# Turning the convolved x: from products with the identity on TensorE to 32-row blocks on VectorE with a DRAM scratch

## The chip, the cores and the metric

The kernel runs on one core of one Trainium2 chip. The metric is the device time of one execution in microseconds (us), the median of several runs. The engines that run side by side on the core are TensorE (PE; its weight loads are listed apart as PEld), VectorE (DVE), ScalarE (ACT), GpSimd (POOL) and SyncE (SP, which here only issues DMAs). Each works through its own queue in order, and a semaphore tells one engine that another is done.

## The reference

A trunk of two layers over 256 tokens of width 2048: first a Mamba-2 SSD mixer, then sliding-window attention, each followed by a layer norm. The change lies in the SSD mixer. Its inner width of 4096 is 8 groups of 8 heads of 64; a chunk is 128 tokens, so there are two.

```python
zxbcdt = x @ w_in                       # z | x, B, C | dt
xbc = silu(causal_conv4(xbc) + conv_b)  # x, B, C
dt = softplus(dt_raw + dt_bias);  a = -exp(a_log)
x_c = xs * dt
y_diag = einsum("bcqgn,bcsgn->bgcqs", c_c, b_c) * decay_in  applied to x_c
y = y_diag + y_off + xs * d_skip
y = y * silu(z);  y = rms_norm over each group of 512 * norm_w
out = y @ w_out
```

`x_c` is summed over tokens s, so TensorE needs x with the tokens on the partitions, while the projection and the convolution give it with the channels on the partitions. That is the turn in question.

## The kernel before

**Weights and units.** All matrix products of the projections are done in fp32 split into a high and a low part (three products: high by high, low by high, high by low). A unit is a weight piece of 128x2048 (1 MB). `load_unit` loads it as two halves `wr` (5 buffers) on SP's queue; ACT writes the high part `wh` (line 133), VectorE subtracts it for the low part `wl` (line 134); 4 buffers each. `next_unit` keeps two units ahead of the one in use. A projection unit is 48 matmuls of 256 columns (lines 195 to 197) into one of 4 PSUM tiles `mm`; an output unit is 24 matmuls of 512 columns (lines 255 to 257) into two of them.

**A group.** `group(g)` runs 10 projection blocks: B, C, four blocks of x, four of z (in group 0 the four z first). Each block's PSUM goes through `conv_silu`: one ACT step (line 357), three taps on VectorE (line 359; the last one frees the PSUM tile), tanh on ACT (362), a closing step on VectorE (363). Between the blocks the output units of the group before are run, four per group. In the program groups take 14 units of 1 MB and 1.5 MB of decay rows.

**The steps of SSD** are put at block numbers of a hand-written plan (`at(t, step)`; t is 10 g plus an offset): `sum_decay` and `exp_decay` make the decays `e` on ACT from rows that a DRAM scratch `rscr` broadcasts; `cb` makes C by B on TensorE and multiplies it into `e` on VectorE; `tr` turns x: eight transposes (products with the identity `ident`, line 453) into two PSUM tiles `ax` and four scaled copies to SBUF tiles `xd` on VectorE (line 458, the scale is `dtx`, dt with a part of the decay); `ymm` computes y with `xd` as the stationary operand and `e` as the moving one (line 476: 16 matmuls of 64 columns, two per head pair side by side, each executed as two weight loads and two matmuls), then VectorE scales by `el` (481) and adds the skip term from `xs` (487); `gate` multiplies by z, squares and sums on POOL and splits y for the output product (506, 507); `norm` follows five blocks later. In groups 2 to 7 `cb` stands at block 4, `tr` at 7, `ymm` at 9. In group 0 they stand at 8, 12 and 13, which is already in group 1's blocks.

**What sets the order.** The plan and the calls give the program order; a scheduler then sets each engine's order from it and from its own estimate of when things are ready. Tiles of one tag share a number of buffers, and a new tile waits until the last reader of the buffer is done.

**Buffers that the change touches.** Tag `sm` has 7 buffers of 1 KB per partition, for the temporaries of `make_dt`, the four `xs` and the squares of `gate`; `xd` has 4 of 1 KB; `yz` one of 4 KB.

Of the kernel before, what the change touches and what calls it, by code (L numbers as in the profile page):

```python
# [8 lines left out]
F32 = mybir.dt.float32  # L9
# [3 lines left out]
ALU = mybir.AluOpType  # L13
AX = mybir.AxisListType

P = 128
S = 256
# [10 lines left out]
TD, TS, CB0 = 5, 5, 8  # L28
# [6 lines left out]

BLOCKS = list(range(10))
BLOCKS0 = [6, 7, 8, 9, 0, 1, 2, 3, 4, 5]
CB_AT, TR_AT, Y_AT, NSM = 4, 7, 9, 7
B_ORDER = [("q", 0), ("g", 0), ("q", 1), ("g", 1), ("o", 0), ("q", 2), ("g", 2), ("o", 1),
           ("q", 3), ("g", 3), ("o", 2), ("o", 3)]  # L40
ALPHA = (2.0 * 2) ** 0.25
# [16 lines left out]
def trunk(ctx: ExitStack, tc: tile.TileContext, A: dict, out: bass.AP, dbg=None):  # L58
    nc = tc.nc
# [12 lines left out]
    dram = pool("dram", space=bass.MemoryType.DRAM)  # L72
# [3 lines left out]
    def nm(s):  # L76
        uid[0] += 1
        return f"{s}_{uid[0]}"
# [4 lines left out]
    def ax_tile():  # L83
        return ax_ps.tile([P, 512], F32, tag="ax", name=nm("ax"), bufs=4)

    cc = cst.tile([P, 896], F32, tag="cc", name="cc")
    ident = cc[:, 0:128]
# [209 lines left out]
    rscr = dram.tile([P, S], F32, tag="rscr", name="rscr")  # L297

    def make_dt(ps):
        f = [ap.tile([P, S], F32, tag="sm", name=nm("f"), bufs=NSM) for _ in range(7)]  # L300
        u, e, rec, z, w, q, dt = [x[:] for x in f]
        nc.scalar.activation(u, ps[:, :S], AF.Identity, bias=pc[:, PC_DTB : PC_DTB + 1])
        nc.scalar.activation(e, u, AF.Abs)
        nc.scalar.activation(e, e, AF.Exp, scale=-1.0)
        aneg = ap.tile([P, 1], F32, tag="aneg", name="aneg")
        nc.scalar.activation(aneg[:], pc[:, PC_ALOG : PC_ALOG + 1], AF.Exp)
        nc.vector.tensor_scalar(aneg[:], aneg[:], -1.0, None, ALU.mult)
        nc.vector.tensor_scalar(rec, e, 2.0, None, ALU.add)
        nc.vector.reciprocal(rec, rec)
        nc.vector.tensor_tensor(z, e, rec, ALU.mult)  # L310
        nc.vector.tensor_tensor(w, z, z, ALU.mult)
        nc.vector.tensor_scalar(q, w, 1.0 / 15.0, None, ALU.mult)
        nc.vector.tensor_scalar(z, z, 2.0, None, ALU.mult)
        for d in (13.0, 11.0, 9.0, 7.0, 5.0, 3.0):
            nc.vector.scalar_tensor_tensor(q, q, 1.0 / d, w, ALU.add, ALU.mult)
        nc.vector.scalar_tensor_tensor(q, q, 1.0, z, ALU.add, ALU.mult)
        nc.vector.scalar_tensor_tensor(dt, u, 0.0, q, ALU.max, ALU.add)
        da, hi = e, rec
        nc.vector.tensor_scalar(da, dt, aneg[:], None, ALU.mult)
        nc.vector.tensor_scalar(hi, da, QUANT, None, ALU.add)  # L320
        nc.vector.tensor_scalar(hi, hi, QUANT, None, ALU.subtract)
# [96 lines left out]
        conv_silu(ps, g * 6 + 1, gs[g].ct[:])  # L418

    def in_xs(g, i, ps):  # L420
        xs = ap.tile([P, S], F32, tag="sm", name=nm("xs"), bufs=NSM)
        conv_silu(ps, g * 6 + 2 + i, xs[:])
        gs[g].__dict__.setdefault("xs", {})[i] = xs

    def in_z(g, i, ps):
        z = ap.tile([P, S], F32, tag="zz", name=nm("z"), bufs=4)
# [15 lines left out]
                e[:], e[:], cbm[:].unsqueeze(1).to_broadcast([P, 4, 384]), ALU.mult  # L442
            )

    def tr(g):
        st = gs[g]
        st.xd = {}
        for k in range(2):
            ps = ax_tile()
            for i in (2 * k, 2 * k + 1):  # L450
                for c in range(2):
                    o = (i % 2) * S + c * P
                    nc.tensor.transpose(ps[:, o : o + P], st.xs[i][:, c * P : (c + 1) * P], ident)
            for i in (2 * k, 2 * k + 1):
                o = (i % 2) * S
                xd = ap.tile([P, 2, 2, 64], F32, tag="xd", name=nm("xd"), bufs=4)
                hh = g * 8 + 2 * i
                nc.vector.tensor_tensor(
                    xd[:], ps[:, o : o + S].rearrange("p (c h d) -> p c h d", c=2, h=2),
                    dtx[:, :, hh : hh + 2].unsqueeze(3).to_broadcast([P, 2, 2, 64]), ALU.mult,  # L460
                )
                st.xd[i] = xd

    def ymm(g):
        st = gs[g]
        st.yz = ap.tile([P, 4, S], F32, tag="yz", name=nm("yz"), bufs=1)
        for k in range(2):
            ps = ax_tile()
            for i in (2 * k, 2 * k + 1):
                o = (i % 2) * S  # L470
                xd = st.xd[i]
                for c in range(2):
                    cols = slice(o + c * P, o + S)
                    for r in range(2):
                        e = es[g, i // 2][:, 2 * (i % 2) + r, :]
                        nc.tensor.matmul(
                            ps[64 * r : 64 * r + 64, cols], xd[:, c, r, :], e[:, 256:] if c else e[:, :256],
                            start=c == 0, stop=c == 1,
                        )
            two = slice(2 * k, 2 * k + 2)  # L480
            nc.vector.tensor_tensor(
                st.yz[:, two, :], ps[:].rearrange("p (i q) -> p i q", i=2), els[g][:, two, :], ALU.mult
            )
            for i in (2 * k, 2 * k + 1):
                col = PC_D + g * 4 + i
                v = st.yz[:, i, :]
                nc.vector.scalar_tensor_tensor(v, st.xs[i][:], pc[:, col : col + 1], v, ALU.mult, ALU.add)  # L487

    def gate(g, i):
        st = gs[g]  # L490
# [103 lines left out]
    def at(t, fn, *a):  # L594
        plan.setdefault(t, []).append((fn, *a))

    at(35, rotary)
    for g in range(NG):
        t = 10 * g
        if g == 0:  # L600
            at(TD, turn_dt, *dts)
            at(TS, load_decay, 0, 1)
            at(TS, load_low, 0)
            steps = TS
            pos = dict(cb=CB0, tr=12, y=13, norm=16)
        elif g == 1:
            at(10, load_decay, 1, 0)
            at(10, load_decay, 1, 1)
            at(13, load_low, 1)
            steps = 13  # L610
            pos = dict(cb=6, tr=TR_AT, y=Y_AT, norm=10 + CB_AT)
        else:
            at(t - 5, load_decay, g, 0)
            at(t - 5, load_decay, g, 1)
            at(t, load_low, g)
            steps = t - 1
            pos = dict(cb=CB_AT, tr=TR_AT, y=Y_AT, norm=10 + CB_AT)
        at(steps, sum_decay, g, 0)
        at(steps + 1, exp_decay, g, 0)
        at(steps + 1, sum_decay, g, 1)  # L620
        at(steps + 2, exp_decay, g, 1)
        at(t + pos["cb"], cb, g)
        at(t + pos["tr"], tr, g)
        at(t + pos["y"], ymm, g)
        for i in range(4):
            at(t + pos["y"], gate, g, i)
        at(t + pos["norm"], norm, g)
# [399 lines left out]
```

## Time and profile before

| what | value |
|---|---|
| runs (3) | median 1022.56 us, 1022.55 to 1023.02 |
| the profiled execution's span, first to last instruction | 1022.1 us |
| mean granted TensorE clock | 0.999 |
| DVE, busiest line: 134, the low parts | 398.3 us in 342 instructions |
| ACT, busiest line: 133, the high parts | 337.4 us in 342 |
| SP's queue (q1) | 192.14 MB, 57.3% of the 16 DMA engines' span |
| line 476 (y) on PE | 128 matmuls of 256 columns, 128 of 128 |
| line 458 (scaled copies) on DVE | 32 instructions, 11.9 us |

A row of the timeline gives the start, the duration, engine, line, operation, what is written and read, the shapes, how many instructions were merged and, in brackets, the idle time of the engine before it with what ended that. "PEq" and "SPq" are the sequencers that issue. Matmuls overlap: the next one starts before the one before it has drained, so the pitch between two starts is the cost of one in a stream, and the duration is longer. A row of a group ends with the busy time, the mean of one in ns, and the idle time before.

### The profile page before, as it was taken

To read this page: it belongs to the slowest core of one execution; us is meant where nothing else is said; L and a number is where in the kernel's file an instruction comes from. 1 tells how busy PE (TensorE), PEld (TensorE's weight loads), DVE (VectorE), ACT (ScalarE), POOL (GpSimd) and SP (SyncE) were. 2 spreads that over 40 slices of the span, in tenths; PEclk is the share of its full clock that TensorE was granted. 3 is DMA by queue.
4 is the path that set the end of the run, shared out by engine and by line. 5 is a ranking of instruction groups with operands and counts; after the bars stand their busy time and mean duration, and the time that the engine had idled before them with its cause. 6 is when DMAs were issued, how large, how long until landed. Compare 5 with 4: busy or idle time off the path is not lost. (4 is left out here: it accounts for less than half of the span.)

```text
span 1022.1 us, 17627 instructions
## 1 busy us (share of the span) xinstructions
PE 1001.7 (98%) x7028; PEld 905.5 (89%) x7028; DVE 774.2 (76%) x1106; ACT 562.8 (55%) x924; POOL 89.8 (9%) x112
## 2 busy tenths in 40 slices
PE   7999999999999999999999999999999999999997
PEld 7999899999998998999999999868988879879975
DVE  6868887876886787696786787798577785785776
ACT  6585857637655655664663763535545453453642
POOL 0000303004003002100300300301000000000002
PEclk9999999999999999999999999999999999999999
DMA  8786676575666666656656556647655445545522
GB/s 308 249 299 246 204 245 195 171 233 169 211 218 191 218 195 204 205 188 202 208 179 218 156 190 210 227 146 232 197 167 169 156 140 183 173 140 183 194 96 82
DMA packets 57794, 199.31 MB, mean 195 GB/s; under 512 B 6304, under 2 KB 10672, under 8 KB 56944
## 3 DMA queue, kind: packets, MB, share of 16 engines
q1 hardware_dynamic: 56352, 192.14, 57.3%
q0 software_dynamic: 1072, 5.53, 1.5%
q8 instruction: 55, 0.90, 0.4%
q10 hardware_dynamic: 288, 0.52, 0.1%
q14 instruction: 27, 0.22, 0.1%
HBM read 195.93 MB, written 2.23 MB: 194 GB/s over the span
## 5 line engine op out<-in xcount | busy, mean ns | idle before, releaser
L134 DVE TENSOR_TENSOR wl<-wr,wh 128x1024 fp32r<-128x1024 f32 (+2 forms) x342 | 398.3, 1181 | 135.4 <-ACT wh L133 134.0
L133 ACT ACTIVATE wh<-wr 128x1024 fp32r<-128x1024 f32 (+2 forms) x342 | 337.4, 1011 | 238.9 <-PE mm L196 77.1
L195 PE MATMUL mm<-xH,wh 128*128 128x256 f32 x1296 | 361.2, 279 | 8.0 <-ACT wh L153 6.0
L197 PE MATMUL mm<-xH,wl 128*128 128x256 f32 x1296 | 359.8, 278 | 2.1 <-DVE wl L134 2.1
L196 PE MATMUL mm<-xL,wh 128*128 128x256 f32 x1296 | 360.1, 278 | 0.0
L195 PEld LDWEIGHTS mm<-xH,wh 128*128 128x128 f32 x1296 | 244.6, 189 | 10.2 <-ACT wh L153 6.3
L197 PEld LDWEIGHTS mm<-xH,wl 128*128 128x128 f32 x1296 | 244.5, 189 | 2.7 <-DVE wl L134 2.7
L196 PEld LDWEIGHTS mm<-xL,wh 128*128 128x128 f32 x1296 | 244.7, 189 | 1.1
L255 PE MATMUL mm<-wh,yH 128*128 128x512 f32 x256 | 101.4, 396 | 0.0
L256 PE MATMUL mm<-wh,yL 128*128 128x512 f32 x256 | 99.9, 390 | 0.0
L257 PE MATMUL mm<-wl,yH 128*128 128x512 f32 x256 | 99.7, 390 | 0.0
L492 POOL TENSOR_TENSOR yz<-yz,z 128x256 f32<-128x256 f32 x32 | 32.9, 1036 | 532.0 <-DVE yz L487 532.0
L195 PE MATMUL mm<-x1H,wh 128*128 128x256 f32 x256 | 71.9, 281 | 0.0
L197 PE MATMUL mm<-x1H,wl 128*128 128x256 f32 x256 | 71.0, 277 | 0.0
L196 PE MATMUL mm<-x1L,wh 128*128 128x256 f32 x256 | 71.0, 277 | 0.0
L359 DVE SCALAR_TENSOR_TENSOR cv<-mm,pc,cv 128x255 f32<-128x255 f32 x144 | 68.6, 476 | 1.4
L712 PE MATMUL mm<-wh,x1H 128*128 128x512 f32 x160 | 63.3, 396 | 0.0
L714 PE MATMUL mm<-wl,x1H 128*128 128x512 f32 x160 | 62.6, 392 | 0.3 <-DVE wl L134 0.2
L713 PE MATMUL mm<-wh,x1L 128*128 128x512 f32 x160 | 62.6, 391 | 0.2 <-DVE x1L L676 0.2
L255 PEld LDWEIGHTS mm<-wh,yH 128*128 128x128 f32 x256 | 48.1, 188 | 10.3 <-DVE z L429 1.0
L257 PEld LDWEIGHTS mm<-wl,yH 128*128 128x128 f32 x256 | 48.1, 188 | 10.2
L256 PEld LDWEIGHTS mm<-wh,yL 128*128 128x128 f32 x256 | 48.1, 188 | 9.0
(180 smaller groups left out, 1306.2 us busy)
## 6 DMA issues: line engine op xcount, KB each, us to landing
wr<-in_wa SPq DMA_DIRECT2D x158, 512.0 KB, 5.0
wr<-in_wo SPq DMA_DIRECT2D x64, 512.0 KB, 4.8
wr<-in_wq SPq DMA_DIRECT2D x32, 512.0 KB, 4.5
wr<-in_wg SPq DMA_DIRECT2D x32, 512.0 KB, 5.2
wr<-in_wb SPq DMA_DIRECT2D x32, 512.0 KB, 4.6
rb<-rscr SPq DMA_DIRECT2D x16, 512.0 KB, 5.4
el<-rscr SPq DMA_DIRECT2D x16, 256.0 KB, 4.8
wr<-in_wkv SPq DMA_DIRECT2D x8, 512.0 KB, 4.3
```

The lines of the kernel that those rows point to most:

```text
L133: nc.scalar.activation(h[:, sl], raw, AF.Copy)
L134: nc.vector.tensor_tensor(l[:, sl], raw, h[:, sl].bitcast(F32), ALU.subtract)
L195: nc.tensor.matmul(ps, ah, bh, start=first, stop=False)
L196: nc.tensor.matmul(ps, ah, bl, start=False, stop=False)
L197: nc.tensor.matmul(ps, al, bh, start=False, stop=last)
L255: nc.tensor.matmul(ps[:], aH[:, k, hs], u.h[:, ks], start=k == 0, stop=False)
L256: nc.tensor.matmul(ps[:], aL[:, k, hs], u.h[:, ks], start=False, stop=False)
L257: nc.tensor.matmul(ps[:], aH[:, k, hs], u.l[:, ks], start=False, stop=k == 3)
L359: nc.vector.scalar_tensor_tensor(a[:, sft:], ps[:, : S - sft], w(3 - sft), a[:, sft:], ALU.mult, ALU.add)
L712: nc.tensor.matmul(ps[:], x1H[:, kk, hs], u.h[:, ks], start=kk == 0, stop=False)
L713: nc.tensor.matmul(ps[:], x1L[:, kk, hs], u.h[:, ks], start=False, stop=False)
L714: nc.tensor.matmul(ps[:], x1H[:, kk, hs], u.l[:, ks], start=False, stop=kk == KT - 1)
```

## The change

`tr` goes away. In its place stand three steps:

- `turn_blocks`: VectorE turns x in blocks of 32x32, two instructions for the four `xs` of a group (one for each chunk), each reading 128x512 and writing 128x512 into `zt`, with consecutive outputs 32 bytes apart. Four stores on SP's queue, one for each 32 partitions, put the blocks into a DRAM scratch `zd` in runs of 1 KB.
- `load_turned`: one load on SP's queue brings 128 x 4 x 1 KB back as `xd`, now with the tokens on the partitions.
- `scale_x`: two products in place with `dtx`, 128x512 each, for the even and the odd heads.

In `ymm` the stationary operand is `st.xv[:, r, :, c, i]`: 64 columns that lie 8 fp32 values (32 bytes) apart, where before they were adjacent. The four `xs` of a group become one tile with a single buffer; `zt` takes the single buffer of `yz`; `sm` goes down to 3 buffers. In groups 2 to 7 the turn stands at block 5, the load at 6, the scale at 8 and `ymm` at 9 as before; in group 0 at 9, 10, 12 and 13.

```diff
-CB_AT, TR_AT, Y_AT, NSM = 4, 7, 9, 7
+CB_AT, ZT_AT, LD_AT, XD_AT, Y_AT, NSM = 4, 5, 6, 8, 9, 3
...
-        f = [ap.tile([P, S], F32, tag="sm", name=nm("f"), bufs=NSM) for _ in range(7)]
-        u, e, rec, z, w, q, dt = [x[:] for x in f]
+        f = [ap.tile([P, S], F32, tag="sm", name=nm("f"), bufs=NSM) for _ in range(3)]
+        f4 = ap.tile([P, 4, S], F32, tag="xs", name=nm("f4"), bufs=1)
+        u, e, rec, z = [f4[:, i, :] for i in range(4)]
+        w, q, dt = [x[:] for x in f]
...
-        xs = ap.tile([P, S], F32, tag="sm", name=nm("xs"), bufs=NSM)
-        conv_silu(ps, g * 6 + 2 + i, xs[:])
-        gs[g].__dict__.setdefault("xs", {})[i] = xs
+        if i == 0:
+            gs[g].xs = ap.tile([P, 4, S], F32, tag="xs", name=nm("xs"), bufs=1)
+        conv_silu(ps, g * 6 + 2 + i, gs[g].xs[:, i, :])
...
-    def tr(g):
+    def turn_blocks(g):
         st = gs[g]
-        st.xd = {}
-        for k in range(2):
-            ps = ax_tile()
-            for i in (2 * k, 2 * k + 1):
-                for c in range(2):
-                    o = (i % 2) * S + c * P
-                    nc.tensor.transpose(ps[:, o : o + P], st.xs[i][:, c * P : (c + 1) * P], ident)
-            for i in (2 * k, 2 * k + 1):
-                o = (i % 2) * S
-                xd = ap.tile([P, 2, 2, 64], F32, tag="xd", name=nm("xd"), bufs=4)
-                hh = g * 8 + 2 * i
-                nc.vector.tensor_tensor(
-                    xd[:], ps[:, o : o + S].rearrange("p (c h d) -> p c h d", c=2, h=2),
-                    dtx[:, :, hh : hh + 2].unsqueeze(3).to_broadcast([P, 2, 2, 64]), ALU.mult,
-                )
-                st.xd[i] = xd
+        zt = ap.tile([P, 4, 32, 2, 4], F32, tag="yz", name=nm("zt"), bufs=1)
+        xv = st.xs[:].rearrange("p i (c b t) -> p c b i t", c=2, b=4)
+        for c in range(2):
+            nc.vector.transpose(zt[:, :, :, c, :].rearrange("p b d i -> p b i d"), xv[:, c, :, :, :])
+        st.zd = dram.tile([4, P, 256], F32, tag="zd", name=nm("zd"), bufs=2)
+        for a in range(4):
+            nc.sync.dma_start(
+                st.zd[a, :, :].rearrange("(b t) f -> t b f", b=4),
+                zt[32 * a : 32 * a + 32, :, :, :, :].rearrange("p b d c i -> p b (d c i)"),
+            )
+
+    def load_turned(g):
+        st = gs[g]
+        st.xd = ap.tile([P, 4, 256], F32, tag="xd", name=nm("xd"), bufs=1)
+        nc.sync.dma_start(st.xd[:], st.zd[:].rearrange("a p f -> p a f"))
+
+    def scale_x(g):
+        st = gs[g]
+        st.xv = st.xd[:].rearrange("p (r a) (d c i) -> p r (a d) c i", r=2, c=2, i=4)
+        dv = dtx[:, :, g * 8 : g * 8 + 8].rearrange("p c (i r) -> p r c i", r=2)
+        for r in range(2):
+            v = st.xv[:, r, :, :, :]
+            nc.vector.tensor_tensor(v, v, dv[:, r, :, :].unsqueeze(1).to_broadcast([P, 64, 2, 4]), ALU.mult)
...
-                            ps[64 * r : 64 * r + 64, cols], xd[:, c, r, :], e[:, 256:] if c else e[:, :256],
+                            ps[64 * r : 64 * r + 64, cols], st.xv[:, r, :, c, i], e[:, 256:] if c else e[:, :256],
...
-            pos = dict(cb=CB0, tr=12, y=13, norm=16)
+            pos = dict(cb=CB0, zt=9, ld=10, xd=12, y=13, norm=16)
...
-        at(t + pos["tr"], tr, g)
+        at(t + pos["zt"], turn_blocks, g)
+        at(t + pos["ld"], load_turned, g)
+        at(t + pos["xd"], scale_x, g)
```

How the instructions stand now, at the places that the prediction speaks of. In the names, `cv` is a conv block in work, `mm` its PSUM tile, `wl`, `wh` and `wr` a unit's low part, high part and raw half; line numbers of the new kernel are larger by 2 (361 for the taps 359, 365 for the closing step 363) or 10 (486 for 476).

VectorE after the last x block of group 0 has been convolved, before the change:

```order
L363 SCALAR_TENSOR_TENSOR xs_945<-xs_945,cv_946 128x256
L359 SCALAR_TENSOR_TENSOR cv_1013<-mm_963,pc,cv_1013 128x255
L134 TENSOR_TENSOR wl_1025<-wr_1028,wh_1024 128x1024
L359 SCALAR_TENSOR_TENSOR cv_1013<-mm_963,pc,cv_1013 128x254
L134 TENSOR_TENSOR wl_1092<-wr_1093,wh_1091 128x1024
L359 SCALAR_TENSOR_TENSOR cv_1013<-mm_963,pc,cv_1013 128x253
L134 TENSOR_TENSOR wl_1092<-wr_1095,wh_1091 128x1024
```

The same place after the change:

```order
L365 SCALAR_TENSOR_TENSOR xs_723<-xs_723,cv_940 128x256
L361 SCALAR_TENSOR_TENSOR cv_1015<-mm_965,pc,cv_1015 128x255
L453 STREAM_TRANSPOSE zt_947<-xs_723 128x4x4x32 x2
L361 SCALAR_TENSOR_TENSOR cv_1015<-mm_965,pc,cv_1015 128x254
L134 TENSOR_TENSOR wl_1029<-wr_1032,wh_1028 128x1024
L361 SCALAR_TENSOR_TENSOR cv_1015<-mm_965,pc,cv_1015 128x253
L134 TENSOR_TENSOR wl_1096<-wr_1097,wh_1095 128x1024
```

The two block turns now stand right behind the first tap of the next block, ahead of the second half of a unit's low part.

VectorE further on, where group 0's x gets its scale, before:

```order
L359 SCALAR_TENSOR_TENSOR cv_1084<-mm_1034,pc,cv_1084 128x253
L363 SCALAR_TENSOR_TENSOR ct_1083<-ct_1083,cv_1084 128x256
L458 TENSOR_TENSOR xd_1163<-ax_1158,dtx 128x256
L458 TENSOR_TENSOR xd_1165<-ax_1158,dtx 128x256
L458 TENSOR_TENSOR xd_1172<-ax_1167,dtx 128x256
L359 SCALAR_TENSOR_TENSOR cv_1151<-mm_1101,pc,cv_1151 128x255
L458 TENSOR_TENSOR xd_1174<-ax_1167,dtx 128x256
L359 SCALAR_TENSOR_TENSOR cv_1151<-mm_1101,pc,cv_1151 128x254
L134 TENSOR_TENSOR wl_1306<-wr_1307,wh_1305 128x1024
L359 SCALAR_TENSOR_TENSOR cv_1151<-mm_1101,pc,cv_1151 128x253
L134 TENSOR_TENSOR wl_1306<-wr_1309,wh_1305 128x1024
```

and after:

```order
L361 SCALAR_TENSOR_TENSOR cv_1088<-mm_1038,pc,cv_1088 128x253
L361 SCALAR_TENSOR_TENSOR cv_1155<-mm_1105,pc,cv_1155 128x255
L365 SCALAR_TENSOR_TENSOR ct_1087<-ct_1087,cv_1088 128x256
L361 SCALAR_TENSOR_TENSOR cv_1155<-mm_1105,pc,cv_1155 128x254
L361 SCALAR_TENSOR_TENSOR cv_1155<-mm_1105,pc,cv_1155 128x253
L134 TENSOR_TENSOR wl_1293<-wr_1294,wh_1292 128x1024
L134 TENSOR_TENSOR wl_1293<-wr_1296,wh_1292 128x1024
L473 TENSOR_TENSOR xd_1022<-xd_1022,dtx 128x512 x2
```

The scale of x used to come before three taps and two low parts; now it comes behind them. On TensorE, y of group 0 used to follow directly on the block `mm_1186`; now the same block is called `mm_1174`, and four matmuls of the block after it (`mm_1302`) stand ahead of y.

SP's queue around group 0's stores and load, before:

```order
L125 DMA wr_1178<-in_wa 128x1024
L125 DMA wr_1180<-in_wa 128x1024
L125 DMA wr_1307<-in_wa 128x1024
L125 DMA wr_1309<-in_wa 128x1024
L125 DMA wr_1384<-in_wo 128x1024
L125 DMA wr_1386<-in_wo 128x1024
```

and after:

```order
L125 DMA wr_1166<-in_wa 128x1024
L125 DMA wr_1168<-in_wa 128x1024
L456 DMA zd_950<-zt_947 32x4x256 x4
L125 DMA wr_1294<-in_wa 128x1024
L125 DMA wr_1296<-in_wa 128x1024
L464 DMA xd_1022<-zd_950 128x4x256
L125 DMA wr_1370<-in_wo 128x1024
L125 DMA wr_1372<-in_wo 128x1024
```

The four stores went in between two units' loads, and the load of the turned x after the first of them.

More of the change, by code (lines that the diff above doesn't have):

```diff
@@ L470, in ymm @@
                 o = (i % 2) * S
-                xd = st.xd[i]
                 for c in range(2):
@@ L486, in ymm @@
                 v = st.yz[:, i, :]
-                nc.vector.scalar_tensor_tensor(v, st.xs[i][:], pc[:, col : col + 1], v, ALU.mult, ALU.add)
+                nc.vector.scalar_tensor_tensor(v, st.xs[:, i, :], pc[:, col : col + 1], v, ALU.mult, ALU.add)
     def gate(g, i):
@@ L610, in trunk @@
             steps = 13
-            pos = dict(cb=6, tr=TR_AT, y=Y_AT, norm=10 + CB_AT)
+            pos = dict(cb=6, zt=ZT_AT, ld=LD_AT, xd=XD_AT, y=Y_AT, norm=10 + CB_AT)
         else:
@@ L616, in trunk @@
             steps = t - 1
-            pos = dict(cb=CB_AT, tr=TR_AT, y=Y_AT, norm=10 + CB_AT)
+            pos = dict(cb=CB_AT, zt=ZT_AT, ld=LD_AT, xd=XD_AT, y=Y_AT, norm=10 + CB_AT)
         at(steps, sum_decay, g, 0)
```

## The prediction

> **What bounds the kernel now.** I read the page first, then the busy time by stretches, then the waits, then the timeline of TensorE and VectorE where group 0 computes its y.
>
> ```profile
> span 1022.1 us, 17627 instructions
> PE 1001.7 (98%) x7028; PEld 905.5 (89%) x7028; DVE 774.2 (76%) x1106; ACT 562.8 (55%) x924; POOL 89.8 (9%) x112
> 70.00:170.00 100.00, 98.16 (x775) 91.92 (x774) 85.06 (x115) 64.00 (x104) 18.72 (x22) 1.00 0.69 222
> 170.00:270.00 100.00, 100.00 (x789) 95.26 (x788) 76.02 (x109) 59.92 (x87) 10.64 (x13) 1.00 0.63 201
> 470.00:570.00 100.00, 100.00 (x750) 92.61 (x749) 75.17 (x99) 57.16 (x89) 12.98 (x16) 1.00 0.63 200
> PE mm L197 <- DVE wl L134: 2.1, 3, 0.8
> ```
>
> The last columns of the stretches are PE, PEld, DVE, ACT, POOL, the granted clock, the DMA share and GB/s. In the eight Mamba groups TensorE never pauses (100.00 of 100 us), VectorE has a quarter of its time free, the DMAs a third. The wait row says that TensorE waited only 2.1 us in all for a weight's low part from VectorE. So a TensorE instruction taken out there is worth its full pitch, and extra VectorE time costs nothing, unless TensorE comes to wait for VectorE at one place. The stretch 70:170 is the weak one: VectorE 85% busy, TensorE not quite full. Group 0's y lies in it.
>
> **What is removed.** Eight transposes per group, 64 in all.
>
> ```profile
> 91.58 0.19 PEld L197 LDWEIGHTS mm<-xH,wl 128*128 128x128 f32 x1
> 91.71 0.89 PEld L453 LDWEIGHTS ax<-cc,xs 128*128 128x128 f32 x8
> 92.57 0.19 PEld L195 LDWEIGHTS mm<-xH,wh 128*128 128x128 f32 x1
> 92.68 0.19 PEld L196 LDWEIGHTS mm<-xL,wh 128*128 128x128 f32 x1
> L453 PE MATMUL ax<-cc,xs 128*128 128x128 f32 x64 | 8.3, 272 | 0.0
> ```
>
> From the weight load before the eight to the one after them 0.99 us pass; between neighbours otherwise 0.11 (92.57 to 92.68). So the eight cost 0.88, and 8 groups 7.0 us. (The group's row says 8.3 busy, because a matmul's tail overlaps the next.) VectorE also loses four scaled copies per group.
>
> **What is added on VectorE.** Two block turns and two products of 128x512 a group, for four products of 128x256.
>
> ```profile
> 300.99 0.76 DVE L458 TENSOR_TENSOR xd<-ax,dtx 128x256 f32<-128x256 f32 x2 [0.85 <-PE ax L453]
> 307.91 1.23 DVE L134 TENSOR_TENSOR wl<-wr,wh 128x1024 fp32r<-128x1024 f32 x1 [2.76 <-ACT wh L133]
> 318.78 1.22 DVE L134 TENSOR_TENSOR wl<-wr,wh 128x1024 fp32r<-128x1024 f32 x1 [3.21 <-ACT wh L133]
> 320.25 1.28 DVE L481 TENSOR_TENSOR yz<-ax,el 128x512 f32<-128x512 f32 x2
> 317.69 0.76 PE L476 MATMUL ax<-e,xd 128*64 128x256 f32 x6
> L309 DVE RECIPROCAL f<-f 128x256 f32<-128x256 f32 x1 | 1.8, 1755 | 0.0
> ```
>
> An elementwise 128x512 takes 0.64 us (two in 1.28). No row shows a block turn. Bounds: 0.64, if it moves an element as fast as a product does; 3.5, if it is as slow as the dearest row per element, the reciprocal (1.755 for 256 columns, doubled). I take 0.64: the turn computes nothing, so the copying rows are nearest. A group then gains 4 x 0.64 and loses 4 x 0.38, 1.0 us net, where VectorE idles 2.8 and 3.2 us just before its subtractions (307.91, 318.78). From group 1 on this is hidden. If that cover were gone, it would be 7 us over seven groups.
>
> **The way through DRAM.** Four stores and one load per group, 1 MB more per group beside some 15 MB, all on SP's in-order queue.
>
> ```profile
> wr<-in_wa SPq DMA_DIRECT2D x158, 512.0 KB, 5.0
> rb<-rscr SPq DMA_DIRECT2D x16, 512.0 KB, 5.4
> rscr<-f SPq DMA_DIRECT2D x2, 64.0 KB, 3.5
> first<-in_first SPq DMA_DIRECT2D x2, 768.0 KB, 9.1
> ```
>
> A store in 1 KB rows (rscr) lands in 3.5 us, a 512 KB load in 5.0 to 5.4, at worst 9.1. Turn, stores, load and products thus take 1.3 + 3.5 + 5.4 + 1.3 = 11.5 us. In a later group, such as the one of the rows above, the old products stand at 300.99 and y's matmuls at 317.69, 16.7 us apart, and by the new order the turn stands ahead of where the old products stood: covered. Behind the stores on SP stand weight loads, and those wait for the subtractions anyway; behind the load, which must wait for all four stores, two weight loads are late by some 1 us at most. The little that TensorE waits for weights (2.1 us in all) says that this prefetch has room. I price it at 0, with 0 to 1 per group as its bounds.
>
> **Group 0 is different**, and here is the price.
>
> ```profile
> 87.95 0.43 DVE L363 SCALAR_TENSOR_TENSOR xs<-xs,cv 128x256 f32<-128x256 f32 x1 [1.31 <-ACT xs L362]
> 88.29 0.48 DVE L359 SCALAR_TENSOR_TENSOR cv<-mm,pc,cv 128x255 f32<-128x255 f32 x1
> 88.69 1.22 DVE L134 TENSOR_TENSOR wl<-wr,wh 128x1024 fp32r<-128x1024 f32 x1
> 89.82 0.48 DVE L359 SCALAR_TENSOR_TENSOR cv<-mm,pc,cv 128x254 f32<-128x254 f32 x1
> ...
> 97.52 0.42 DVE L363 SCALAR_TENSOR_TENSOR ct<-ct,cv 128x256 f32<-128x256 f32 x1 [0.55 <-ACT ct L362]
> 97.86 1.08 DVE L458 TENSOR_TENSOR xd<-ax,dtx 128x256 f32<-128x256 f32 x3
> 98.33 2.58 PEld L476 LDWEIGHTS ax<-e,xd 128*64 128x64 f32 x32 [0.23 <-DVE xd L458]
> 123.92 0.39 PE L257 MATMUL mm<-wl,yH 128*128 128x512 f32 x1
> 125.63 0.35 PE L195 MATMUL mm<-xH,wh 128*128 128x256 f32 x1 [1.32 <-DVE cv L359]
> 125.01 0.47 DVE L359 SCALAR_TENSOR_TENSOR cv<-mm,pc,cv 128x253 f32<-128x253 f32 x1
> ```
>
> Here VectorE works without a pause from 88.29, and TensorE already waits 0.23 us for xd at 98.33. By the new order VectorE has, after the tap at 88.29 and up to the second product: 9 taps at 0.40 (88.29 to 88.69), 7 subtractions at 1.13 (88.69 to 89.82), 2 closing steps at 0.34 (87.95 to 88.29), 2 turns and 2 products at 0.64. That is 3.6 + 7.9 + 0.7 + 1.3 + 1.3 = 14.8, so the products end at 103.0. (The load is there by then: the turn ends at 90.0, the stores land at 93.5, and the load, if issued at 94, is there at 99.4, 2.3 us ahead of the products.) TensorE comes to y at 98.33 - 0.23 - 0.88 + 0.45 = 97.7, the last term being the four matmuls now ahead of it. It then stands still for 103.0 - 97.7 = 5.3 us, and all later matmuls stand behind y in its queue.
>
> Part of this comes back. At 123.92 TensorE loses 1.5 us (1.71 to the next start, 0.23 of it the normal pitch), because a PSUM buffer is freed by a tap that VectorE does at 125.01. TensorE now comes 5.3 - 0.23 - 0.88 = 4.2 us later there; the work that leads to the tap hangs on group 0's y only in part (the decays and xs on ACT). Bounds: the tap is late by 4.2 too, nothing is regained; or by at most 2.7, and 1.5 us are. I take 1.5, since by the new order ACT does that conv's first step one weight conversion sooner.
>
> **The strided weights of y.** The stationary operand's 64 columns now lie 32 bytes apart.
>
> ```profile
> L476 PEld LDWEIGHTS ax<-e,xd 128*64 128x64 f32 x256 | 16.0, 137 | 5.7 <-DVE xd L458 0.2
> L476 PE MATMUL ax<-e,xd 128*64 128x128 f32 x128 | 12.4, 273 | 0.0
> L197 PEld LDWEIGHTS mm<-xH,wl 128*128 128x128 f32 x1296 | 244.5, 189 | 2.7 <-DVE wl L134 2.7
> ```
>
> 64 columns load in 137 ns, 128 in 189: 0.81 ns a column, 52 ns a load. All 32 instructions take 2.75 us (98.33 to 101.08), 16 pairs (two head halves side by side), with the 128-column ones half as long as the 256-column ones: about 108 and 215 ns a pair. A load twice as slow (104) still hides under 108. Bounds: 0, and, at four times, 208 - 108 = 0.1 us on 8 pairs in 8 groups, 6.4 us. I take 0.
>
> **The sum** against the profiled 1022.1: -7.0 - 0.2 + 5.3 - 1.5 = -3.4, so 1018.7; the median of the runs (1022.56) lies 0.46 above that execution, so **1019.2 us**.
>
> **Rivals.**
>
> (1) The pause in group 0 costs the clock as well.
>
> ```profile
> 6.63 0.41 PE L196 MATMUL mm<-xL,wh 128*128 128x256 f32 x1
> 6.84 0.41 PE L197 MATMUL mm<-xH,wl 128*128 128x256 f32 x1
> 8.96 0.58 PE L195 MATMUL mm<-xH,wh 128*128 128x256 f32 x1 [1.70 <-ACT wh L153]
> 13.24 0.28 PE L195 MATMUL mm<-xH,wh 128*128 128x256 f32 x1
> 13.35 0.28 PE L196 MATMUL mm<-xL,wh 128*128 128x256 f32 x1
> ```
>
> At the start matmuls follow each other at 0.21 us (6.63 to 6.84), and from 13.24 on at 0.11, though the granted clock reads full speed. Pauses up to 1.3 us (125.63) leave the pace. One of 5.3 us is longer than any after the start; if it brings the half pace back for the 4.3 us from 8.96 to 13.24, half of that, 2.1, is lost: 1021.3. [...]
>
> (2) The other side: the strided weight load. Its place is y's 8 short pairs; it decides once a load is over twice as slow, or if a pair's two loads go one after the other. Price 6.4: 1025.6. Against it: 0.81 ns a column leaves slack. [...] No row here has such a load.
>
> (3) Also slower: the turn is as slow as the reciprocal. Group 0's pause grows by 2 x 2.9 = 5.7, the clock falls: 1027.0.
>
> (4) Group 0's pause does not come, because ACT or the loads, not VectorE's list, set the old times: 1022.56 - 7.2 = 1015.4. Against it: VectorE's rows leave no gap from 88.29 on.
>
> (5) The change does nothing on the clock: what the transposes free is lost to waits for PSUM or the prefetch: 1022.6. Against it: the stretches at 100.00.
>
> **Chances.** Forecast 0.34, (1) 0.23, (2) 0.14, (3) 0.13, (4) 0.08, (5) 0.08. A measurement tells 0.2%, 2.0 us. Faster: the forecast, (4) and the early edge of (1), 0.46. Same: the rest of (1), (5), the early edge of (3), 0.28. Slower: (2) and most of (3), 0.26. Range 1016.5 to 1026.5: it leaves out (4) and the far half of (3).
>
> **What would show it.** In the new profile: no eights of transposes, a group's pitch from group 2 on 0.88 us shorter; a pause of TensorE of about 5 us near 97.7, ended by VectorE's product; no pause near 124; the turn at 0.7 us; y's 32 instructions at 2.75 us in later groups. Wrong, if y's take over 3.4 us, if the pause is below 3 or above 8 us, if TensorE waits for xd in any later group, or if matmuls after the pause run at 0.21.

## The result, and the profile after

The changed kernel takes 1024.47 us (median of 20 runs, 1022.35 to 1027.08), the kernel before 1022.51 us beside it (20 runs, 1019.61 to 1025.81). The ratio is 1.0019, with a 95% interval of 1.001 to 1.0027: slower by some 2 us, where 3.4 us of gain were forecast. The time lies inside the range of the prediction, but on the other side of no change.

The page of the changed kernel, its busy time by stretches (PE, PEld, DVE, ACT, POOL, then granted clock, DMA share, GB/s), TensorE's waits and the groups that are new:

```profile
span 1022.2 us, 17573 instructions
PE 999.0 (98%) x6964; PEld 905.7 (89%) x6964; DVE 788.7 (77%) x1106; ACT 563.6 (55%) x924; POOL 90.5 (9%) x112
```

```profile
70.00:170.00 100.00, 94.70 (x725) 89.66 (x724) 87.03 (x112) 60.44 (x96) 18.96 (x22) 0.97 0.74 239
95.00:135.00 40.00, 34.80 (x266) 33.11 (x265) 34.08 (x47) 28.88 (x48) 9.80 (x11) 0.91 0.69 223
470.00:570.00 100.00, 100.00 (x747) 93.64 (x746) 76.83 (x100) 57.17 (x88) 12.76 (x16) 1.00 0.68 215
```

```profile
PE ax L486 <- DVE xd L473: 5.2, 1, 5.2
```

```profile
L486 PEld LDWEIGHTS ax<-e,xd 128*64 128x64 f32 x256 | 23.3, 207 | 7.3 <-DVE xd L473 5.4 <-issue 0.2
L453 DVE STREAM_TRANSPOSE zt<-xs 128x512 f32<-128x512 f32 x16 | 17.6, 1173 | 0.5
L473 DVE TENSOR_TENSOR xd<-xd,dtx 128x512 f32<-128x512 f32 x16 | 10.4, 688 | 3.4 <-DMA xd<-zd 3.4
```

The 64 transposes are gone (7028 matmuls to 6964) and TensorE is still full in the later groups (100.00 of 100 us). One stretch stands out: from 95 to 135 us the granted clock is 0.91, and one wait of 5.2 us stands there. The block turn took 1.17 us where 0.64 was taken, and a weight load of y 207 ns where it was 137.

Group 0 on TensorE's and VectorE's timelines (start, duration, instruction), and y of group 2 on TensorE's:

```profile
95.90 0.28 PE L195 MATMUL mm<-xH,wh 128*128 128x256 f32 x1
101.37 5.00 PE L486 MATMUL ax<-e,xd 128*64 128x256 f32 x32 [5.20 <-DVE xd L473]
106.31 0.38 PE L196 MATMUL mm<-xL,wh 128*128 128x256 f32 x1
```

```profile
86.21 0.48 DVE L361 SCALAR_TENSOR_TENSOR cv<-mm,pc,cv 128x255 f32<-128x255 f32 x1
86.60 2.18 DVE L453 STREAM_TRANSPOSE zt<-xs 128x512 f32<-128x512 f32 x2
...
98.36 2.35 DVE L134 TENSOR_TENSOR wl<-wr,wh 128x1024 fp32r<-128x1024 f32 x2
100.63 1.28 DVE L473 TENSOR_TENSOR xd<-xd,dtx 128x512 f32<-128x512 f32 x2
```

```profile
237.07 2.97 PE L486 MATMUL ax<-e,xd 128*64 128x256 f32 x32
239.97 0.50 PE L255 MATMUL mm<-wh,yH 128*128 128x512 f32 x1
```

The way through DRAM, by the DMA issues (KB each, us to landing):

```profile
zd<-zt SPq DMA_DIRECT2D x32, 128.0 KB, 2.8
xd<-zd SPq DMA_DIRECT2D x8, 512.0 KB, 6.7
```

VectorE goes from the tap at 86.21 through its list to the products, whose second ends at 100.63 + 1.28 = 101.91, and no row in between shows it waiting for x's load (issued at 92.8 us and landed 6.8 us later, at 99.6, a microsecond ahead of the products). TensorE has nothing to do from 95.90 on. Then y's 32 instructions take 4.94 us (101.37 to 106.31); in the later groups they take 2.90 (237.07 to 239.97), 2.75 before.

The spans of single executions differ already ahead of the first place that the change touches: TensorE waits there for the first converted weights (7.6 us in all in the profile of the kernel before), for longer in one execution than in another, and group 0's first C B matmul starts at 66.1 to 69.4 us in all kernels that leave it in its place. From that matmul to the end of the span the kernel before took 953.62 us, and 953.64 in a second profile; single rows of the table below differed by up to 0.64 us between those two profiles (29.83 and 29.59, 82.24 and 81.90, 389.54 and 390.18) and cancelled in the sum. So the two kernels are held against each other from there, by the starts of y's first matmul in each group (us):

| stretch | before | after | difference | forecast |
|---|---|---|---|---|
| first C B matmul (68.50; 67.16) to y of group 0 | 29.83 | 34.22 | +4.39 | +4.6 |
| y of group 0 to y of group 1 | 55.68 | 54.94 | -0.74 | -2.8 |
| y of group 1 to y of group 2 | 81.44 | 80.75 | -0.69 | -0.88 |
| y of group 2 to y of group 3 | 82.24 | 82.93 | +0.69 | -0.88 |
| y of group 3 to y of group 6 | 244.32 | 242.25 | -2.07 | -2.64 |
| y of group 6 to y of group 7 | 70.57 | 69.85 | -0.72 | -0.88 |
| y of group 7 to the end | 389.54 | 390.09 | +0.55 | 0 |
| sum | 953.62 | 955.03 | +1.41 | -3.4 |

The forecast column is the prediction's sum laid out by place: 5.3 - 0.23 - 0.88 + 0.45 in the first row, -1.5 - 0.88 - 0.45 in the second. The 0.45 are four projection matmuls that the changed kernel runs ahead of group 0's y and the kernel before behind it: 244 and 240 of them lie between C B and that y, and 284 and 288 between it and y of group 1. Two rows went wrong above all, the second by 2.1 us and the fourth by 1.6, and each later group gave 0.16 to 0.19 less than forecast.

The last row is no sign of the change: the program's last four matmuls took 1.98 us in this profile of the kernel before and 3.78 in that of the changed one:

```profile
1014.46 1.98 PE L916 MATMUL ax<-t,dg 128*128 128x512 f32 x4 [0.89 <-ACT dg L906]
```

```profile
1013.92 3.78 PE L928 MATMUL ax<-t,dg 128*128 128x512 f32 x4 [0.89 <-ACT dg L918]
```

In the second profile of the kernel before they took 3.68 us, and its last row 390.18.

The fourth row was not on the list at all. In group 2 VectorE waits for the small load of the rotary tables, and 30 us later TensorE waits for a PSUM buffer, which a tap frees. The rows are VectorE's and TensorE's before, then VectorE's and TensorE's after:

```profile
251.51 0.17 DVE L575 CAST posf<-posi 128x2 f32<-128x2 int32 x1 [2.71 <-DMA posi<-in_pos]
...
283.89 0.36 PE L195 MATMUL mm<-xH,wh 128*128 128x256 f32 x1 [0.57 <-DVE cv L359]
```

```profile
254.90 0.17 DVE L585 CAST posf<-posi 128x2 f32<-128x2 int32 x1 [4.47 <-DMA posi<-in_pos]
...
287.05 0.35 PE L195 MATMUL mm<-xH,wh 128*128 128x256 f32 x1 [1.53 <-DVE cv L361]
```

The load took 2.12 us to land before and 3.88 after; VectorE's wait grew from 2.71 to 4.47 and TensorE's from 0.57 to 1.53.

### The profile page after: what moved, and what is told of

Its sections match the earlier page's. It is cut to its first block, busy times and chain, and to the rows that moved or that the text cites. A ratio compares the mean times of both kernels' runs of the same rounds, so it can differ in the third digit from the quotient of the medians.

```text
span 1022.2 us, 17573 instructions
## 1 busy us (share of the span) xinstructions
PE 999.0 (98%) x6964; PEld 905.7 (89%) x6964; DVE 788.7 (77%) x1106; ACT 563.6 (55%) x924; POOL 90.5 (9%) x112
## 4 chain that ended last, share of the span: by engine, by line
PE 78%; DVE 9%; ACT 4%; DMA 4%; issue 3%; POOL 1%; SPq 0%; DVEq 0%; ACTq 0%; POOLq 0%
PE mm L195 14%; PE mm L196 14%; PE mm L197 14%; PE mm L255 7%; PE mm L257 7%; PE mm L256 7%; DVE wl L134 3%; PE mm L724 3%; PE mm L725 3%; PE mm L726 3%; PE ax L486 2%; ACT wh L133 2%; DMA wr<-in_wo 1%; DMA wr<-in_wa 1%; PE ax L816 1%
```

## The experiments

Each kernel is the changed one with the edit shown, unless said otherwise. Ratios are to the kernel before, run on the same chip beside it, with their 95% intervals; "the stretch" is one row of the table above.

### Group 0 on TensorE

```diff
-        at(t + pos["zt"], turn_blocks, g)
-        at(t + pos["ld"], load_turned, g)
-        at(t + pos["xd"], scale_x, g)
+        if g == 0:
+            at(12, tr0)
+        else:
+            at(t + pos["zt"], turn_blocks, g)
+            at(t + pos["ld"], load_turned, g)
+            at(t + pos["xd"], scale_x, g)
```

(`tr0` is the old turn: eight transposes on TensorE, four scaled copies on VectorE, and weights of 64 adjacent columns)

> Group 0 alone turns its x on TensorE as before (8 transposes, 4 scaled copies, weights of 64 adjacent columns); groups 1 to 7 keep the change. Theory A (the loss sits in group 0's pause): against the changed kernel the pause of 5.2 us and the half pace of y behind it (4.94 for 2.75 us) go, the transposes' 0.88 and the PSUM wait of 1.5 near 124 us come back: -5.2 - 2.2 + 0.9 + 1.5 = -5.0, so 1019.5 us, faster than before. Theory B (the loss is spread over the later groups: strided weights, a fuller VectorE, a fuller DMA queue): 1023.5 to 1024.5. Theory C (the half pace is not the pause's but y's own): 1021.7, and no slow y to be seen here.

Measured: 1017.32 us, ratio 0.9951 (0.9932 to 0.9969). TensorE at y of group 0:

```profile
96.35 0.28 PE L197 MATMUL mm<-xH,wl 128*128 128x256 f32 x1
96.56 2.82 PE L505 MATMUL ax<-e,xd 128*64 128x256 f32 x32
99.31 0.39 PE L195 MATMUL mm<-xH,wh 128*128 128x256 f32 x1
...
131.76 0.50 PE L255 MATMUL mm<-wh,yH 128*128 128x512 f32 x1 [1.02 <-DVE xr L262]
```

No pause, y in 2.75 us, granted clock 1.00. A PSUM wait of 1.02 us returned at 131.76, as expected in kind. Theory A holds and theory B falls: seven turned groups are a gain. In the profile 7.2 us went: 5.0 before y of group 0, 0.4 behind it, 1.4 in the stretch from group 2 to group 3, 0.4 at the end. The expectation had missed the third, and the last is the end of the program, which differs from run to run as said above.

### Group 0's y one block later

```diff
-            pos = dict(cb=CB0, zt=9, ld=10, xd=12, y=13, norm=16)
+            pos = dict(cb=CB0, zt=9, ld=10, xd=12, y=14, norm=16)
...
-            at(13, load_low, 1)
-            steps = 13
+            at(14, load_low, 1)
+            steps = 14
```

> The changed kernel with group 0's y matmuls one block later (and group 1's decay steps with them). Theory A (TensorE only came too early; VectorE's list ends at 102 and a block is 5.5 us): the pause shrinks to under 0.5 us and y runs at 2.9 us; -5.2 - 2.2 + 1.5 for a PSUM wait that returns = -5.9, so 1018.6 us (1017 to 1019.5). Rival (VectorE, 85% busy from 70 to 170 us, is the bound there, and its backlog only shows at another place): a wait of 3 to 5 us of TensorE for a tap, a decay or a weight's low part follows within the next two blocks, 1022 to 1024.5.

Measured: 1021.96 us, ratio 0.9990 (0.9977 to 1.0003): 3.0 us less than the changed kernel by the ratios, where theory A gave 5.9. The pause before y is gone, but TensorE's timeline shows another, at group 0's norm:

```profile
117.01 0.28 PE L197 MATMUL mm<-xH,wl 128*128 128x256 f32 x1
119.39 0.67 PE L526 MATMUL ax<-cc,sq 128*128 128x1 f32 x4 [2.10 <-POOL sq L508]
...
121.20 0.77 PE L255 MATMUL mm<-wh,yH 128*128 128x512 f32 x1
121.77 0.63 PE L256 MATMUL mm<-wh,yL 128*128 128x512 f32 x1
122.20 0.63 PE L257 MATMUL mm<-wl,yH 128*128 128x512 f32 x1
122.62 0.63 PE L255 MATMUL mm<-wh,yH 128*128 128x512 f32 x1
123.05 0.47 PE L256 MATMUL mm<-wh,yL 128*128 128x512 f32 x1
123.36 0.39 PE L257 MATMUL mm<-wl,yH 128*128 128x512 f32 x1
123.59 0.40 PE L255 MATMUL mm<-wh,yH 128*128 128x512 f32 x1
```

y had moved by a block and its norm had not, so the norm's matmuls came 2.1 us before POOL's sum of squares was ready. Behind that wait the matmuls ran at half pace until 123.36: a 512-column one every 0.43 us, 0.23 from there on. The same rows of the changed kernel, at full pace:

```profile
122.36 0.50 PE L526 MATMUL ax<-cc,sq 128*128 128x1 f32 x4
...
124.61 0.39 PE L257 MATMUL mm<-wl,yH 128*128 128x512 f32 x1
```

From the norm to the sixth output matmul that is 2.25 us there, and 3.97 here (119.39 to 123.36): the half pace cost 1.7 us on top of the 2.1 of the wait. The rival named a new wait too, but of VectorE's making; this one is POOL's.

### The norm one block later as well

```diff
-OUT_AT = [[], [6, 7, 8, 9]] + [[4, 6, 8, 9]] * 5 + [[7]]
+OUT_AT = [[], [7, 8, 9]] + [[4, 6, 8, 9]] * 5 + [[7]]
...
-            pos = dict(cb=CB0, zt=9, ld=10, xd=12, y=13, norm=16)
+            pos = dict(cb=CB0, zt=9, ld=10, xd=12, y=14, norm=17)
```

(with group 1's steps at 14, as in the run before)

> The kernel with group 0's y one block later, and now its norm one block later too, with group 1's first output unit moved behind it (three units inside the group and one at its end, for four inside). In the run with y later, TensorE stood 2.1 us before the norm's matmuls at 117.01 for POOL, and the matmuls from 119.39 to 123.36 ran at about half pace (a 512-column matmul at 0.43 for 0.23 us). Theory A (that wait and the half pace behind it, some 2.1 + 2.0 us, are what ate the gain): neither is left, 1021.96 - 4.1 + 1.2 for a PSUM wait near 124 that may return = 1017.9 to 1019.1 us. Rival (VectorE's backlog): another wait of 2 us or more in group 1, 1021 or more.

Measured: 1017.17 us, ratio 0.9944 (0.9931 to 0.9956). TensorE is busy for all of the stretch that was the weak one:

```profile
95.00:135.00 40.00, 40.00 (x317) 38.09 (x316) 38.33 (x51) 29.63 (x49) 9.26 (x11) 1.00 0.74 232
```

From y of group 0 to y of group 2 it takes 129.11 us (42.92 + 86.19), the run before 133.02 (52.27 + 80.75): 3.9 less, against the 2.1 + 1.7 read off above. VectorE has no backlog that must come out somewhere; TensorE was only sent to y a block too early.

### Matmuls that fill the pause

```diff
+        if g == 0:
+            idle = ax_tile()
+            for _ in range(40):
+                nc.tensor.matmul(idle[:, :S], xH(0, 1)[:, 0, :P], xH(0, 1)[:, 0, :], start=True, stop=True)
         for k in range(2):
             ps = ax_tile()
```

> The changed kernel with 40 matmuls of 128x256 more ahead of group 0's y, into a PSUM buffer that nobody reads; they fill 40 x 0.114 = 4.6 of the 5.2 us in which TensorE waits. Theory A (the pause costs the clock, and the half pace of y is that cost): y starts at the same place and takes 2.9 instead of 4.94 us, granted clock 1.00 there: -2.0, 1022.4 us. Rival (y of group 0 is slow for its loads or for the DMA traffic beside it): 4.94 us as in the changed kernel, 1024.5.

Measured: 1022.84 us, ratio 1.0000 (0.9986 to 1.0015). The granted clock stays at full, and y, again just behind a wait for xd, is faster:

```profile
95.00:135.00 40.00, 39.31 (x318) 37.67 (x317) 33.65 (x49) 27.71 (x47) 8.79 (x11) 1.00 0.71 230
```

```profile
104.03 3.56 PE L490 MATMUL ax<-e,xd 128*64 128x256 f32 x32 [0.69 <-DVE xd L473]
107.52 0.38 PE L195 MATMUL mm<-xH,wh 128*128 128x256 f32 x1
```

So the half pace is the pause's doing, and the rival falls: the same loads of the same weights take 3.49 us instead of 4.94. The stretch from y of group 0 to y of group 1 became only 0.8 us shorter (54.94 to 54.13), not 2.0. Of the difference, 0.45 is order: with the filling the four projection matmuls stand behind y again (288 in the stretch, for 284). For equal work the stretch gained 1.3 us. Another 1.7 of this profile came from the stretch of the rotary load (82.93 to 81.23), which the edit does not touch. What is left above 2.90 us is no clock: y starts when the first of the two products is done, and its second matmul waits for the other (in the changed kernel, where the products end at 101.91, the two start at 101.37 and 101.87). In the run with the norm later, with full clock and no wait on record, y still took 3.34 us:

```profile
100.33 3.41 PE L486 MATMUL ax<-e,xd 128*64 128x256 f32 x32
103.67 0.39 PE L195 MATMUL mm<-xH,wh 128*128 128x256 f32 x1
```

By the ratios the edit gave 1.9 us (1.0019 to 1.0000), as expected in sum, though not from the place expected; the two intervals overlap, so the ratios alone do not show a gain.

### The rotary load elsewhere, in both kernels

```diff
+    def rotary_in():
         posi = ap.tile([P, 2], I32, tag="posi", name="posi")
...
+    def rotary():
+        posi, inv = pin
...
+    at(25, rotary_in)
     at(35, rotary)
```

> The changed kernel with the two small loads of the rotary tables (8 KB in all) issued ten blocks sooner, so that VectorE no longer waits 4.5 us for them in group 2's last blocks. Theory A (this wait, and TensorE's 1.6 us near 285 us behind it, were made longer by the change's own stores and loads and belong to its loss): 81.44 - 0.69 = 80.75 us from y of group 2 to y of group 3 instead of 82.93, and 1.5 to 2.2 us less than the changed kernel: 1022.6. Rival (the wait is in the kernel before too, 0.8 us there, and its length is the chance of a run): the same 0.8 us as the same edit gives on the kernel before, 1023.6.

> The kernel before with the same two loads ten blocks sooner: the control for the run beside it. y of group 2 to y of group 3 falls from 82.24 to 81.44 us: -0.8, 1021.8 us, if that stretch only; no change if TensorE then waits elsewhere.

Measured: 1022.78 us, ratio 0.9995 (0.9986 to 1.0003), for the changed kernel; 1022.88 us, ratio 0.9996 (0.9984 to 1.0008), for the kernel before. The wait did not go, since VectorE's steps moved along with the load. In the changed kernel:

```profile
173.79 0.17 DVE L591 CAST posf<-posi 128x2 f32<-128x2 int32 x1 [3.10 <-DMA posi<-in_pos]
```

It now costs 0.46 us between groups 1 and 2 (81.21 for 80.75) instead of 2.18 between groups 2 and 3. From y of group 1 to y of group 3 the changed kernel gains 1.7 us (163.68 to 161.96), the kernel before 0.2 (163.68 to 163.50). The two kernels then stand at the same ratio, and against 1.0019 the edit gave the changed kernel 0.24%, 2.5 us (from the two intervals some 1 to 4), where the control gained 0.4 by its ratio. So in the changed kernel this wait cost about as much as the whole loss.

A second profile of the kernel before asked whether that is chance:

> The kernel before, unchanged, for a second profile of it. In its first profile the rotary load took 2.12 us to land and TensorE lost 0.8 us from y of group 2 to y of group 3 (82.24 for 81.44); in seven profiles of kernels with the change at that place it took 2.14, 2.54, 3.28, 3.58, 3.58, 3.84 and 3.88 us and TensorE lost 0.5 to 2.2. If the change makes the load slow: near 2.1 us and 82.2 us again. If it is chance: any value up to 3.9 us, and with 3.5 or more a stretch of 83.1 us or more.

```profile
251.99 0.17 DVE L575 CAST posf<-posi 128x2 f32<-128x2 int32 x1 [2.70 <-DMA posi<-in_pos]
```

VectorE's wait is 2.70 us again, and the stretch 81.90. That makes 2.7 us in both profiles of the kernel before, and 2.7 to 4.5 in the seven changed kernels with the load at its old place. One of the seven, the filled pause, had the short wait too (2.73 us, and 0.5 lost in the stretch). It leans to the change, but two profiles against seven do not show it; why the load lands later stays open, since the transfers in flight beside it are the same two, before and after: a weight load issued 2.9 us ahead of it and a decay load issued 1.0 us behind it.

### Filling the pause, with the rotary load moved

The 40 matmuls of above are 46 here, and the rotary loads stand as in the run above.

> The changed kernel with the rotary loads ten blocks sooner, and 46 matmuls into an unread PSUM buffer ahead of group 0's y, which fill 46 x 0.12 = 5.5 us of TensorE's wait. To be held against the same kernel without them (ratio 0.9995 to before). Theory (the pause costs the clock 1.5 us from y of group 0 to y of group 1, 55.06 us there): 53.5 us with them, granted clock 1.00 from 95 to 135 us, and 1.2 to 1.5 us less in all: ratio 0.998. Rival (half pace has another cause): 55.06 us again, ratio 0.9995 or more.

Measured: 1021.97 us, ratio 0.9991 (0.9982 to 1.0001). The granted clock is 1.00 from 95 to 135 us, and the stretch from y of group 0 to y of group 1 takes 54.18 us instead of 55.06: 0.9 less, and 1.3 for equal work, since here too four matmuls of 0.45 us moved behind y. The ratio moves the right way by 0.0004, less than its interval can tell. The clock's share of the loss is thus 1.3 us in both fillings, at the place where 1.5 were expected; filling the pause gives back 0.8 to 0.9 of it, since the four matmuls had been free inside the pause.

### Blocks written in runs of 32 values

```diff
-        zt = ap.tile([P, 4, 32, 2, 4], F32, tag="yz", name=nm("zt"), bufs=1)
+        zt = ap.tile([P, 4, 2, 4, 32], F32, tag="yz", name=nm("zt"), bufs=1)
...
-            nc.vector.transpose(zt[:, :, :, c, :].rearrange("p b d i -> p b i d"), xv[:, c, :, :, :])
+            nc.vector.transpose(zt[:, :, c, :, :], xv[:, c, :, :, :])
...
-                            ps[64 * r : 64 * r + 64, cols], st.xv[:, r, :, c, i], e[:, 256:] if c else e[:, :256],
+                            ps[64 * r : 64 * r + 64, cols], st.xw[:, r, 4 * c + i, :], e[:, 256:] if c else e[:, :256],
```

(the products write `xw`, out of place, with 64 adjacent columns a head)

> The changed kernel with the turned blocks written in runs of 32 adjacent values instead of single values 32 bytes apart, and the products writing y's weights as 64 adjacent columns (4 products of 256 for 2 of 512). Theory A (the stride is what made the turn 1.17 us and y's later groups 2.90): a turn at 0.64 to 0.70, y at 2.75 in groups 1 to 7 (-1.05 us), group 0's chain of turn, stores, load and products 0.8 us shorter: -1.9, 1022.6 us. Rival for the turn (1.17 is the block turn's own price, two clocks a value): 1.17 again, then -1.0, 1023.5. Rival for the weights (the 0.15 us a group is not the stride's): y stays at 2.90.

Measured: 1022.42 us, ratio 0.9995 (0.9984 to 1.0007). The groups of the turn and of y's weight loads:

```profile
L453 DVE STREAM_TRANSPOSE zt<-xs 128x512 f32<-128x512 f32 x16 | 10.5, 690 | 0.5
L488 PEld LDWEIGHTS ax<-e,xw 128*64 128x64 f32 x256 | 18.9, 147 | 9.5 <-DVE xw L475 4.2 <-issue 0.2
```

Both strides were at fault, and both rivals fall: the turn takes 0.69 us, as long as the elementwise product of that size (688 ns in the changed kernel), a weight load 147 ns, and y of a later group 2.75 us (235.77 to 238.52). A later group's pitch is 80.58 us, 0.86 under the 81.44 of before, where 0.88 was forecast for the transposes. Group 0's pause shrank from 5.20 to 3.98 us, but y behind it took 5.43 us.

### x's blocks first in group 0

```diff
+SEQ0 = [0, 1, 2, 6, 7, 8, 9, 4, 5, 3]
...
-            pos = dict(cb=CB0, zt=9, ld=10, xd=12, y=13, norm=16)
+            pos = dict(cb=10, zt=7, ld=8, xd=10, y=13, norm=16)
```

(`SEQ0` sets the order of group 0's blocks and of their weights)

> The changed kernel with group 0's blocks in another order: x's four after three of z, then B, C and the last of z, so that the turn, the way through DRAM and the products come two to three blocks sooner; group 0's C B product two blocks later, y where it was. All eight groups turn on VectorE. Theory A (group 0's xd is late because its x comes last in the group, and not for VectorE's load as such): no pause before y, y at 2.9 us: -5.2 - 1.5 + 1.2 for a PSUM wait that returns near 124 = -5.5, 1019.0 us; without that wait 1017.8. Rival (VectorE has too much to do until 100 us, whatever the order): TensorE waits 3 us or more for the decays, for C B or for a weight's low part instead, 1022 to 1025.

Measured: 1015.81 us, ratio 0.9928 (0.9912 to 0.9944), better than expected. On TensorE:

```profile
94.94 2.97 PE L487 MATMUL ax<-e,xd 128*64 128x256 f32 x32
97.84 0.38 PE L196 MATMUL mm<-xH,wh 128*128 128x256 f32 x1
```

All eight groups turn on VectorE, there is no pause, and y of group 0 takes 2.90 us like the others. VectorE does the same work as in the changed kernel, so its load as such was not the cause: the place of x in group 0 was.

### The repairs together

> The three repairs in one kernel: group 0 on TensorE, blocks written in runs of 32 with adjacent weights, rotary tables loaded sooner. If they add up: 1017.3 (group 0 on TensorE) - 7 x 0.15 for the weights - 0.8 for the rotary wait = 1015.5 us, ratio to before 0.993; groups 4 to 7 at a pitch of 80.58 us, 80.58 from y of group 2 to y of group 3 too. Rival (what one repair frees another wait takes): 1017.3 again.

> All eight groups turn on VectorE, in runs of 32 with adjacent weights, x's blocks of group 0 first, rotary loads sooner. If the parts add: x first alone gave a ratio of 0.9928 to before; 8 x 0.15 = 1.2 us less for y's weights and 1.0 less for the rotary wait give 0.9906, 1013 us beside a before of 1022.6. Rival (the shares overlap with waits that stay, as the PSUM wait near 129 and the rotary wait that only moves by a group): 0.992.

Measured: 1015.38 us, ratio 0.9922 (0.991 to 0.9933), with group 0 on TensorE; 1014.32 us, ratio 0.9924 (0.9906 to 0.9942), with x first. Both beat the kernel before by 0.8%, and the changed kernel by 0.95%. The first came out as the sum of its parts, with 80.58 us in groups 3 to 6. The second did not reach its 0.9906: its weights gave what they should (80.58 too), but TensorE still lost 1.4 us between groups 1 and 2 (81.97 for 80.58), where the rotary load had gone, and waited 1.19 us for PSUM near 129 us. By their intervals these two and x first alone are not told apart.

## Why the prediction was wrong, step by step

- **What bounds the kernel, and the gain per transpose: right.** 0.86 of 0.88 us a group came, once nothing else was in the way (80.58 for 81.44). From 170 to 570 us TensorE stayed at 100.00 of 100 us, but for the stretch from 270 to 370 us with the PSUM wait behind the rotary load (98.28; 99.43 before).
- **Group 0's pause: right as a wait; the size came out right in part by luck.** Forecast 5.3 us, ended by VectorE's product; measured 5.2. VectorE's list was as counted (seven subtractions, nine taps, two turns, two products). It ran 15.7 us from the first tap to the end (86.21 to 101.91) where 14.8 were worked out, mostly since the two turns took 2.18 instead of 1.3. Two things made up for it, and neither was in the sum: y starts on the first product, half a microsecond before the second is done (101.37 and 101.91), and TensorE itself came half a microsecond later than worked out.
- **The PSUM wait near 124 us: right.** It is gone in the changed kernel, and one of 1.0 us came back where the pause was taken away.
- **The clock at 0: wrong.** This was rival (1), and it happened: granted clock 0.91 from 95 to 135 us. It was priced at 2.1 us; the fillings put it at 1.3 for equal work. Some 0.6 us more was lost as y began on one product and waited for the other (3.49 us at full clock, for 2.90). With 0.15 for the weights these make up 2.0 of the 2.1 us by which the second row of the table missed. A shorter gap brought half pace too: a wait of 2.1 us, with four one-column matmuls behind it, was enough in the run with y later (a 512-column matmul every 0.43 us, for 0.23).
- **The strided weights at 0: wrong in size.** 0.15 us a group, 1.2 us in all (2.90 for 2.75). That is far from rival (2)'s 6.4, so the slack that was read off the pairs was real, but not enough for a load of 207 ns in place of 137; with adjacent columns (147 ns) the 0.15 were gone.
- **The turn at 0.64 us: wrong as used.** It holds for adjacent writes (0.69), not for values 32 bytes apart (1.17). Outside group 0 it was hidden, as forecast.
- **The way through DRAM at 0 in later groups: right at the place that was looked at.** Stores of 2.8 and a load of 6.7 us, for 3.5 and 5.4 taken, and y never waited for xd there; VectorE's own waits for that load, 3.4 us in all, held up no matmul of y. The prediction did not weigh the new loads and stores against the small transfers beside them, and the rotary load is the other row that missed: 1.4 us between groups 2 and 3 in the profile (82.93 for the 81.55 that 0.69 less would give), some 1 to 4 by the ratios of moving it. That the change made that load late is likely, not shown.

From -3.4 to +1.4 us in the profiles, row by row: 0.2 gained up to y of group 0, 2.1 lost behind it (clock 1.3, second product 0.6, weights 0.15), 1.1 in the six later groups' stretches at 0.16 to 0.19 a group, 1.4 beside that for the rotary load, and 0.55 behind y of group 7. The last is within what that stretch does from run to run (389.1 to 390.2 us in all profiles, both kernels), by the pace of the last four matmuls above all. The largest step that failed is pricing the pause as idle time alone: the forecast of a gain rested on a pause of 5.3 us that cost nothing more than itself, where 1.9 us came on top. The strided weights at 0 (1.2 us over eight groups) and the way through DRAM at 0 (1.4, if the rotary load belongs to it) are the other two; none of the three alone is the whole miss.

## What to carry to other kernels

Work taken off the bounding engine paid its pitch here only where its replacement was ready (0.86 of 0.88 us in a later group, a wait of 5.2 us in group 0): check the first iteration apart from the steady ones, and if the new path is longer there, move the consumer, its followers and their other inputs by the same step. Price a pause of TensorE with the slow matmuls behind it (1.3 us behind 5.2 here, 1.7 behind 2.1), and lay a replaced operand out so that its readers and writers keep adjacent values (a turn of 0.69 us for 1.17, a weight load of 147 ns for 207). Where single executions scatter by more than the effect, compare stretches between fixed instructions, and count that the same work lies between them: four matmuls that changed sides hid a third of the clock's price here. Take a second profile of the same kernel to see what a row is worth: the steady rows agreed to 0.01 us, others differed by up to 0.64.

## What the runs showed of the hardware beyond that

- A wait of 2.1 us on TensorE was followed by 4.0 us of half pace (119.39 to 123.36), at a cost of 1.7 us; before the change a wait of 1.3 us at the PSUM buffer was followed by matmuls at 0.11 to 0.12 us, full pace. The length of one wait does not settle it: at the end of the program four matmuls behind a wait of 0.89 us took 1.98 us in the profile of the kernel before and 3.78 in that of the changed one.
- A block turn of 128x512 in fp32 takes 0.69 us with 32 adjacent values on the writing side and 1.17 us with values 32 bytes apart.
- A weight load of 64 columns 32 bytes apart is 207 ns instead of 137, 2.2 us more over the 32 loads of a group, and still mostly hidden: y takes 0.15 us longer (2.90 for 2.75).
- The load of the rotary positions, two values a partition, landed after 2.1 to 3.9 us, and 1.8 us of extra wait on VectorE was still 1.0 us of extra wait on TensorE 30 us later. Between the two, VectorE's waits for ScalarE were much the same in both kernels (1.7 us once, then mostly 0.5 a turn), so the delay was not made up.
